# Reciprocal roots of norms, delta rule outputs and latent attention as one GpSimd power each

## The chip, the cores and the metric

One core of a Trainium2 chip runs the whole program. Its engines work side by side, each through its own list of instructions in order, and wait for one another by semaphores: TensorE (PE) multiplies matrices, VectorE (DVE) and ScalarE (ACT) do elementwise work, GpSimd (POOL) does elementwise work too, SyncE (SP) issues most of the DMAs. The metric is the time of one execution in microseconds on the device; lower is better.

## The reference

A trunk of two layers over 512 tokens of width 1024, all in fp32. Each layer adds a half-step feed-forward block, two token mixers side by side (a gated delta rule with 8 heads, and latent attention with 8 heads), and a second half-step feed-forward block. Root-mean-square norms stand everywhere:

```python
def rms_norm(x, gain):
    xf = x.astype(jnp.float32)
    y = xf * lax.rsqrt(jnp.mean(xf * xf, axis=-1, keepdims=True) + EPS)
    return (y * gain.astype(jnp.float32)).astype(x.dtype)
...
def gated_deltanet(qkv, z, ...):
    q, k = l2_norm(q), l2_norm(k)
    o = gated_delta_rule(q, k, v, g, beta)
    o = rms_norm(o, out_gain) * jax.nn.silu(z)
...
    t_inv = lax.linalg.triangular_solve(eye + m, ...)
...
def mla(...):
    q = (rms_norm(q_lat, q_lat_gain) @ w_q_up)
    kv = (rms_norm(kv_lat, kv_lat_gain) @ w_kv_up)
    q, k = rms_norm(q, q_norm), rms_norm(k, k_norm)
...
    for l in range(DEPTH):
        h = modulate(x, norm_ffn1[l], sh1, sc1)
        x = x + 0.5 * (1.0 + g1) * swiglu(h, ...)
        h = modulate(x, norm_mix[l], sh2, sc2)
        x = x + (1.0 + g2) * token_mix(h, ...)
        h = modulate(x, norm_ffn2[l], sh3, sc3)
        x = x + 0.5 * (1.0 + g3) * swiglu(h, ...)
```

## The kernel before

Activations lie feature by feature: 1024 features are 8 tiles of 128 partitions by 512 tokens. Every fp32 product is made of three matmuls (L94) of split operands: high by high, low by high, high by low. A weight slab arrives by DMA as `raw`, ScalarE rounds it to `whi` (L121), and VectorE subtracts that to get `wlo` (L122). A projection of 512 columns into the PSUM tile `acc` (three buffers) is 24 matmuls; behind it VectorE empties the accumulator, in the mixer with a causal convolution of three rows at L729 into `cv`.

The order of each engine's instructions is set by a scheduler that works through the program with priorities; a few stretches are pinned to the order of the code (the beginning, and the matmuls of some norms). So an edit that makes one row longer or shorter can change the order of other rows too.

Where reciprocal roots stand:

- **Begin** (L1446 to L1451). The first norm of the program: PE sums squares into `sm`, VectorE makes the variance `nv`, then a ScalarE square root, a VectorE reciprocal and one Newton round; PE spreads the result into `po`.
- **Norms** (`norm_scale`). Five later norms, each in two halves of 256 tokens. PE puts the sums of squares into `sm`, VectorE makes `nv` (128x2), `rsqrt` makes the root, PE spreads it into `po`. Between the two PE runs matmuls of a neighbouring projection.
- **Block inverse** (`invert`, once a layer). Before it, `key_system` runs once for each of the 8 heads: GpSimd adds a mask (L821) and multiplies (L823), VectorE forms `M` (L840), GpSimd copies its diagonal blocks (L842). GpSimd also makes the rotary products of the key (L1101 to L1122, tile `kr`). Then VectorE transposes the blocks (L855) and runs a forward substitution of 31 steps, each a product at L861 and a subtraction at L863. Meanwhile PE runs projections, whose accumulators VectorE empties between those steps. The tile `nh` (L1312 to L1315, 128x32) is the root of the keys' squared norms, made as a value times its reciprocal root; it is first used after the inverse.
- **Delta rule** (`gdn_tail`, 16 times: 8 heads, 2 layers). `sso` is the outputs' mean square, `som` its reciprocal root (128x4); the outputs `osb` are multiplied by it, transposed by PE and gated. The next head's chain of products with copies on VectorE (L1005, L1014) runs beside it.
- **Latent attention** (`mla_make`, 8 times: 4 pairs of heads, 2 layers). `ss` holds the mean squares of queries and keys, `scl` the 16 reciprocal roots; the key tiles `A` are scaled (L1202) and transposed by PE into `sm` (L99). The makes of pairs 1 to 3 stand within the attention of the pair ahead. The latent norm's root `rkv` (128x4) is made once a layer.

`rsqrt` without a table takes ten VectorE rows: a first guess from the bits of the number (L334) and three Newton rounds (L337 to L339). With a table it is a ScalarE square root (L331), a VectorE reciprocal (L332) and one round.

Of the kernel before, what the change touches and what calls it, by code (L numbers as in the profile page):

```python
# [62 lines left out]

BUFS = {
# [3 lines left out]
}  # L68

# [4 lines left out]
class Trunk:  # L74
# [119 lines left out]
    def setup(self):  # L194
        nc = self.nc
        self.one = self.t("ones", [P, 1])
        nc.vector.memset(self.one, 1.0)
        self.ones = self.one[:].to_broadcast([P, P])
        self.x = self.t("M", [P, KT, SEQ])
        self.condb = self.t("kph", [P, D])  # L200
        for k in range(0, KT, 2):
            nc.sync.dma_start(self.x[:, k:k + 2, :], self.ap["x"][:, k:k + 2, :])
        ct = self.t("ct", [P, KT])
        nc.sync.dma_start(ct, self.ap["c"])
        nc.sync.dma_start(self.condb, self.ap["crow"].to_broadcast([P, D]))
        self.cond = self.t("cond", [P, KT])
        self.const = self.t("const", [P, N_CONST])
        self.ident = self.const[:, C_ID:C_ID + P]
        self.neg = self.const[:, C_NEG:C_NEG + P]
        self.negt = self.const[:, C_NEGT:C_NEGT + P]  # L210
        nc.sync.dma_start(self.ident, self.ap["consts"][:, C_ID:C_ID + P])
        return ct
# [110 lines left out]
            nc.scalar.activation(sq[:, a:b], self.x[:, k, a:b], AF.Square)  # L323
            nc.vector.tensor_add(self.ss[:, a:b], self.ss[:, a:b], sq[:, a:b])

    def rsqrt(self, out, a, table=True):

        nc = self.nc
        n = out.shape[-1]
        if table:  # L330
            nc.scalar.activation(out, a, AF.Sqrt)  # L331
            nc.vector.reciprocal(out, out)  # L332
        else:
            nc.vector.tensor_scalar(out.bitcast(I32), a.bitcast(I32), -0.5, float(0x5F3759DF), ALU.mult, ALU.add)  # L334
        t = self.t("nr", [P, NI])[:, :n]
        for _ in range(1 if table else 3):
            nc.vector.scalar_tensor_tensor(t, out, -0.5, out, ALU.mult, ALU.mult)  # L337
            nc.vector.tensor_mul(t, t, a)
            nc.vector.scalar_tensor_tensor(out, t, 1.5, out, ALU.add, ALU.mult)  # L339

    def norm_scale(self, cols):

        nc = self.nc
        a, b = cols
        n = (b - a) // P
        ps = self.p("sm", [P, n, P])
        for i in range(n):
            self.mm(ps[:, i, 0:1], self.ss[:, a + i * P:a + (i + 1) * P], self.one, start=True, stop=True)
        var, rn = self.t("nv", [P, NT])[:, :n], self.t("nv", [P, NT])[:, :n]
        nc.vector.tensor_scalar(var, ps[:, :, 0], 1.0 / D, EPS, ALU.mult, ALU.add)  # L350
        self.rsqrt(rn, var, False)
        yield
        rb = self.p("po", [P, n, P])
        for i in range(n):
            self.mm(rb[:, i, :], rn[:, i:i + 1].to_broadcast([P, P]), self.ident, start=True, stop=True)
        yield rb[:].rearrange("p t c -> p (t c)")
# [674 lines left out]
    def gdn_tail(self, vec, st):  # L1031
# [3 lines left out]
        a, m = st["sso"], self.t("som", [P, NT])  # L1035
        nc.vector.tensor_scalar(ssq, ssq, EPS, EPS * P, ALU.add, ALU.mult)
        nc.vector.scalar_tensor_tensor(a, a, 1.0 / P, ssq, ALU.mult, ALU.add)
        self.rsqrt(m[:], a[:], False)
        nc.vector.tensor_mul(osb, osb, m[:].unsqueeze(2).to_broadcast([P, NT, P]))
        yield  # L1040
        ot = self.p("po")
# [83 lines left out]
    def mla_make(self, l, pr, lat, mla, st):  # L1125
# [59 lines left out]
        nc.vector.tensor_mul(ss[:, 1], ss[:, 1], b2(mla["rkv2"][:]))  # L1185
        nc.vector.tensor_add(ss[:, 1], ss[:, 1], b2(mla["kpe"][:]))
        scl = self.t("scl", [P, 2, NT, 2])
        self.rsqrt(scl[:].rearrange("p a t h -> p (a t h)"), ss[:].rearrange("p a t h -> p (a t h)"), False)
        nc.vector.tensor_scalar(scl[:, 0], scl[:, 0], QK ** -0.5, None, ALU.mult)
        rk = self.t("rk", [P, NT, 2])  # L1190
        nc.vector.tensor_mul(rk, scl[:, 1], b2(mla["rkv"][:]))
# [75 lines left out]
    def mix(self, l, vec, gate, finish, ws, ahead):  # L1267
# [42 lines left out]

        nh = gt["nh"]
        nc.vector.tensor_scalar(nh, gt["ssk"], 4.0 * EPS, None, ALU.add)  # L1312
        rs = self.t("s1", [P, NI])
        self.rsqrt(rs[:], nh[:])
        nc.vector.tensor_mul(nh, nh, rs)  # L1315
        tt = self.t("A", [P, NI, P])
        for i, _ in enumerate(self.invert(mall, diag, tt)):
            self.fill(FILL_INVERT[i])
# [109 lines left out]
    def begin(self, ct, vec, mod):  # L1428
# [13 lines left out]
        ordered(nc.scalar.activation(self.cond, ct, AF.Silu))  # L1442
        ordered(nc.scalar.activation(self.condb, self.condb, AF.Silu))
        nc.scalar.dma_start(self.ap["spill_c"], self.condb)
        var, rn, t = (self.t(n, [P, NT]) for n in ("nv", "nv", "nr"))
        ordered(nc.vector.tensor_scalar(var, ps[:, :, 0], 1.0 / D, EPS, ALU.mult, ALU.add))  # L1446
        ordered(nc.scalar.activation(rn, var, AF.Sqrt))
# [3 lines left out]
        ordered(nc.vector.scalar_tensor_tensor(rn, t, 1.5, rn, ALU.add, ALU.mult))  # L1451
# [218 lines left out]
```

## Time and profile before

| what | value |
|---|---|
| three runs, us | 2736.4, 2739.33, 2739.42 |
| median, us | 2739.33 |
| the profiled execution, us | 2742.08 |
| its span, us | 2740.3 |
| mean granted clock of TensorE | 0.998 |
| DMA over the span | 394.66 MB, 144 GB/s |

The span is what the profile's rows cover, from the first to the last instruction; the execution's own time lies 1.8 us above it. A row of the timeline gives the start and the length in microseconds, the engine, the line, the operation, the output and its inputs, and in brackets the idle time of that engine ahead of the row and what ended it. Where a matmul is concerned, starts are more exact than ends.

The steps of a root as they stand in the trace of before:

```profile
L337 DVE SCALAR_TENSOR_TENSOR nr<-som x48: 152/161/239, 585.1 to 2092.7; 128x4 f32<-128x4 f32 x48
L337 DVE SCALAR_TENSOR_TENSOR nr<-nv x30: 149/161/164, 378.0 to 2394.7; 128x2 f32<-128x2 f32 x30
L337 DVE SCALAR_TENSOR_TENSOR nr<-scl x24: 165/172/177, 750.2 to 2256.3; 128x16 f32<-128x16 f32 x24
L337 DVE SCALAR_TENSOR_TENSOR nr<-s x2: 192/192/192, 471.8 to 1828.0; 128x32 f32<-128x32 f32 x2
```

The three numbers are the shortest, the median and the longest duration in ns: a step takes some 0.16 us for up to 4 columns and 0.19 for 32.

### The profile page before, as it was taken

What the parts mean: (1) busy time and instruction counts of PE and PEld (TensorE: products, weight loads), DVE (VectorE), ACT (ScalarE), POOL (GpSimd) and SP (SyncE); (2) the same over time, 40 slices, a digit from 0 to 9 for tenths busy, and PEclk for the clock granted to TensorE, in tenths of its full rate; (3) what the DMA queues carried; (4) which work ended last, traced back from release to release, by engine and by line L of the source; (5) the groups of instructions that cost most, each with busy time, mean ns of one, the idle gap of its engine ahead of it and who ended that gap; (6) DMA issues with size and microseconds to landing.
All of it is one profiled execution on the core that took longest, in us unless ns stands there. A gap on an engine that the chain in (4) does not pass through costs nothing.

```text
span 2740.3 us, 44511 instructions
## 1 busy us (share of the span) xinstructions
PE 2695.0 (98%) x17168; PEld 2396.7 (87%) x17168; DVE 2006.5 (73%) x4025; ACT 1285.4 (47%) x2519; POOL 266.9 (10%) x390
## 2 busy tenths in 40 slices
PE   7999999999999999999999999999999999999999
PEld 6989988788888788998889999887888888898988
DVE  6877877777668767875678878786767686685755
ACT  5534345444446535443445344545434564453533
POOL 0000015000001011000010000150000111110000
PEclk9999999999999999999999999999999999999999
DMA  8678733222222453885528777322222224456642
GB/s 308 184 224 236 239 125 111 90 69 81 67 79 71 131 177 114 247 232 146 158 67 229 244 231 235 97 100 89 74 81 71 76 78 125 156 153 185 161 131 86
DMA packets 118869, 394.66 MB, mean 144 GB/s; under 512 B 13440, under 2 KB 16128, under 8 KB 118656
## 3 DMA queue, kind: packets, MB, share of 16 engines
q1 hardware_dynamic: 106128, 350.38, 38.7%
q0 software_dynamic: 10080, 36.70, 7.5%
q10 hardware_dynamic: 2448, 4.72, 0.4%
q8 instruction: 135, 2.21, 0.3%
q14 instruction: 78, 0.64, 0.1%
HBM read 376.55 MB, written 15.20 MB: 143 GB/s over the span
## 4 chain that ended last, share of the span: by engine, by line
PE 82%; DVE 9%; issue 3%; ACT 3%; POOL 2%; DMA 1%; SPq 0%; ACTq 0%; POOLq 0%; DVEq 0%
PE acc L94 57%; PE sc L94 16%; PE sm L94 5%; PE sm L99 2%; DVE wlo L122 2%; PE po L94 1%; DVE cv L729 1%; DVE L L861 1%; DVE L L863 1%; POOL g L821 0%; ACT whi L121 0%; POOL g L823 0%; POOL O L842 0%; DMA raw<-in_w_in 0%; ACT hhi L389 0%
## 5 line engine op out<-in xcount | busy, mean ns | idle before, releaser
L121 ACT CAST whi<-raw 128x512 fp32r<-128x512 f32 (+2 forms) x554 | 320.0, 607 | 429.2 <-PE acc L94 241.1
L94 PE MATMUL acc<-hhi,whi 128*128 128x512 f32 (+1 forms) x1368 | 506.3, 371 | 11.1 <-DVE cv L729 5.8
L94 PE MATMUL acc<-hlo,whi 128*128 128x512 f32 (+1 forms) x1368 | 487.6, 357 | 1.2 <-POOL hlo L392 0.3
L94 PE MATMUL acc<-hhi,wlo 128*128 128x512 f32 (+1 forms) x1368 | 486.7, 356 | 0.0
L122 DVE TENSOR_TENSOR wlo<-raw,whi 128x512 fp32r<-128x512 f32 (+2 forms) x554 | 387.9, 719 | 107.8 <-ACT whi L121 101.0
L94 PE MATMUL acc<-O,whi 128*128 128x512 f32 x1472 | 456.3, 391 | 2.7 <-ACT O L135 2.2
L94 PE MATMUL acc<-A,whi 128*128 128x256 f32 (+1 forms) x1808 | 346.6, 291 | 0.7 <-ACT g L653 0.5
L94 PEld LDWEIGHTS acc<-O,whi 128*128 128x128 f32 x1472 | 275.9, 188 | 60.4 <-ACT O L135 2.6
L94 PEld LDWEIGHTS acc<-hhi,whi 128*128 128x128 f32 x1368 | 259.5, 190 | 42.4 <-issue 8.3
L94 PEld LDWEIGHTS acc<-hhi,wlo 128*128 128x128 f32 x1368 | 259.4, 190 | 37.3 <-DVE wlo L1491 0.2
L94 PEld LDWEIGHTS acc<-A,whi 128*128 128x128 f32 x1808 | 286.0, 192 | 6.2 <-ACT g L653 0.9
L94 PEld LDWEIGHTS acc<-hlo,whi 128*128 128x128 f32 x1368 | 260.3, 190 | 31.7 <-POOL hlo L392 3.0
L94 PE MATMUL acc<-O,wlo 128*128 128x512 f32 x736 | 287.3, 390 | 0.0
L94 PE MATMUL acc<-A,wlo 128*128 128x256 f32 (+1 forms) x904 | 262.6, 290 | 0.0
L582 ACT CAST whi<-L 128x1024 fp32r<-128x1024 f32 x140 | 147.0, 1050 | 205.0 <-issue 77.0
L583 DVE TENSOR_TENSOR wlo<-L,whi 128x1024 fp32r<-128x1024 f32 x140 | 171.3, 1224 | 35.3 <-ACT whi L582 34.6
L94 PEld LDWEIGHTS acc<-A,wlo 128*128 128x128 f32 x904 | 173.3, 192 | 2.5
L269 DVE SCALAR_TENSOR_TENSOR L<-L,kph 128x1024 f32<-128x1024 f32 x142 | 169.9, 1220 | 5.0 <-DMA L<-in_ada_w 5.0
L583 DVE TENSOR_TENSOR wlo<-raw,whi 128x1024 fp32r<-128x1024 f32 x105 | 128.6, 1224 | 59.1 <-ACT whi L582 58.1
L557 POOL DMA_DIRECT2D L<-in_ffn_w x70 | 61.1, 873 | 1086.0 <-DMA L<-in_ffn_w 459.7
L582 ACT CAST whi<-raw 128x1024 fp32r<-128x1024 f32 x105 | 110.2, 1049 | 118.9 <-PE acc L94 49.3
L94 PEld LDWEIGHTS acc<-O,wlo 128*128 128x128 f32 x736 | 138.5, 188 | 28.9
(432 smaller groups left out, 5339.5 us busy)
## 6 DMA issues: line engine op xcount, KB each, us to landing
raw<-in_ffn_w SPq DMA_DIRECT2D x166, 512.0 KB, 4.3
L<-in_ada_w SPq DMA_DIRECT2D x142, 512.0 KB, 5.0
raw<-in_w_in SPq DMA_DIRECT2D x108, 512.0 KB, 3.4
L<-in_ffn_w SPq DMA_DIRECT2D x105, 512.0 KB, 4.5
L<-in_ffn_w POOLq DMA_DIRECT2D x70, 512.0 KB, 8.4
raw<-in_w_branch_a SPq DMA_DIRECT2D x16, 512.0 KB, 3.4
raw<-in_w_branch_b SPq DMA_DIRECT2D x16, 512.0 KB, 3.7
raw<-in_w_out SPq DMA_DIRECT2D x16, 512.0 KB, 3.5
```

Source lines behind the costliest of these rows:

```text
L94: i = self.nc.tensor.matmul(*a, **k)
L99: i = self.nc.tensor.transpose(*a, **k)
L121: nc.scalar.copy(hi[:, s], raw[:, s])
L122: nc.vector.tensor_sub(lo[:, s], raw[:, s], hi[:, s].bitcast(F32))
L269: self.order(self.nc.vector.scalar_tensor_tensor(raw, raw, 1.0, self.condb, ALU.mult, ALU.mult, accum_out=mod[:, o:o + 1]))
L557: nc.gpsimd.dma_start(t, w13[l, m2, half2].rearrange("p w k c -> p (w k c)"), accum_op=ALU.add)
L582: nc.scalar.copy(hi, t)
L583: nc.vector.tensor_sub(lo, t, hi[:].bitcast(F32))
L729: nc.vector.scalar_tensor_tensor(acc[:, s:], ps[:, :SEQ - s], w[j], acc[:, s:], ALU.mult, ALU.add)
L861: nc.vector.tensor_mul(tv, f[:, j + 1:, j:j + 1].to_broadcast([P, n, w]), x[:, j:j + 1, :w].to_broadcast([P, n, w]))
L863: nc.vector.tensor_sub(x[:, j + 1:, :w], x[:, j + 1:, :w], tv)
```

## The change

`rsqrt` becomes a single GpSimd `tensor_tensor` with the operation power, whose second operand is a constant -0.5 broadcast from a new tile `power`; VectorE fills that tile once at the start. The roots of `begin` go the same way, and `nh` becomes a power with +0.5. There are 39 powers: 1 of 128x4 at the beginning, 10 of 128x2 in the norms, 2 of 128x32 for `nh`, 16 of 128x4 for the delta rule, 2 of 128x4 for the latents, and 8 of 128x16 for attention. VectorE's list falls from 3711 to 3335 rows, GpSimd's grows from 347 to 386, ScalarE loses 6 (square roots and their table loads). The work buffers `nr` go.

```diff
+        self.power = self.t("power", [P, 2])
+        nc.vector.memset(self.power[:, 0:1], -0.5)
+        nc.vector.memset(self.power[:, 1:2], 0.5)
...
-    def rsqrt(self, out, a, table=True):
-
-        nc = self.nc
-        n = out.shape[-1]
-        if table:
-            nc.scalar.activation(out, a, AF.Sqrt)
-            nc.vector.reciprocal(out, out)
-        else:
-            nc.vector.tensor_scalar(out.bitcast(I32), a.bitcast(I32), -0.5, float(0x5F3759DF), ALU.mult, ALU.add)
-        t = self.t("nr", [P, NI])[:, :n]
-        for _ in range(1 if table else 3):
-            nc.vector.scalar_tensor_tensor(t, out, -0.5, out, ALU.mult, ALU.mult)
-            nc.vector.tensor_mul(t, t, a)
-            nc.vector.scalar_tensor_tensor(out, t, 1.5, out, ALU.add, ALU.mult)
+    def rsqrt(self, out, a):
+
+        self.nc.gpsimd.tensor_tensor(out, a, self.power[:, 0:1].to_broadcast([P, a.shape[-1]]), ALU.pow)
...
         nc.vector.tensor_scalar(nh, gt["ssk"], 4.0 * EPS, None, ALU.add)
-        rs = self.t("s1", [P, NI])
-        self.rsqrt(rs[:], nh[:])
-        nc.vector.tensor_mul(nh, nh, rs)
+        nc.gpsimd.tensor_tensor(nh, nh, self.power[:, 1:2].to_broadcast([P, NI]), ALU.pow)
...
-        var, rn, t = (self.t(n, [P, NT]) for n in ("nv", "nv", "nr"))
+        var, rn = (self.t("nv", [P, NT]) for _ in range(2))
         ordered(nc.vector.tensor_scalar(var, ps[:, :, 0], 1.0 / D, EPS, ALU.mult, ALU.add))
-        ordered(nc.scalar.activation(rn, var, AF.Sqrt))
-        ordered(nc.vector.reciprocal(rn, rn))
-        ordered(nc.vector.scalar_tensor_tensor(t, rn, -0.5, rn, ALU.mult, ALU.mult))
-        ordered(nc.vector.tensor_mul(t, t, var))
-        ordered(nc.vector.scalar_tensor_tensor(rn, t, 1.5, rn, ALU.add, ALU.mult))
+        self.rsqrt(rn, var)
```

The other three calls of `rsqrt` lose only their `False`. The lines of the changed kernel are lower by 8 in the functions behind `rsqrt` (L813 and L815 are the old L821 and L823, L834 the old L842).

The scheduler orders several engines anew. First GpSimd in layer 0, ahead of the block inverse. Before:

```order
L821 TENSOR_TENSOR g_4664<-g_4664,const_73 128x512
L1121 TENSOR_TENSOR g_4691<-g_3987,g_4680 128x4x32
L1122 TENSOR_TENSOR kr_4686<-kr_4686,g_4691 128x256
L823 TENSOR_TENSOR g_4664<-g_4664,kap_4039 128x512
L842 COPY O_4043<-M_4042 32x128 x4
```

And of the change, at the same place:

```order
L813 TENSOR_TENSOR g_4642<-g_4642,const_76 128x512
L1113 TENSOR_TENSOR g_4669<-g_3965,g_4658 128x4x32
L1305 TENSOR_TENSOR nh_4019<-nh_4019,power_63 128x32
L1114 TENSOR_TENSOR kr_4664<-kr_4664,g_4669 128x256
L815 TENSOR_TENSOR g_4642<-g_4642,kap_4017 128x512
L834 COPY O_4021<-M_4020 32x128 x4
```

The power of `nh` now stands ahead of the product at L815, whose result VectorE needs for the last `M`, and so ahead of the copies that the transpose waits for.

Second, VectorE up to the first group of convolutions within the substitution. The width of a step (175, 192, ...) tells how far the substitution has come. Before:

```order
L861 TENSOR_TENSOR L_4710<-L_4708,L_4709 128x156
L863 TENSOR_TENSOR L_4709<-L_4709,L_4710 128x26x6
L122 TENSOR_TENSOR wlo_4854<-raw_4852,whi_4853 128x512
L729 SCALAR_TENSOR_TENSOR cv_4801<-acc_4766,vec_75,cv_4801 128x509
L861 TENSOR_TENSOR L_4710<-L_4708,L_4709 128x175
```

And of the change, from the same point of the substitution:

```order
L853 TENSOR_TENSOR L_4681<-L_4679,L_4680 128x156
L855 TENSOR_TENSOR L_4680<-L_4680,L_4681 128x26x6
L122 TENSOR_TENSOR wlo_4780<-raw_4778,whi_4779 128x512
L853 TENSOR_TENSOR L_4681<-L_4679,L_4680 128x175
L855 TENSOR_TENSOR L_4680<-L_4680,L_4681 128x25x7
L853 TENSOR_TENSOR L_4681<-L_4679,L_4680 128x192
L855 TENSOR_TENSOR L_4680<-L_4680,L_4681 128x24x8
L853 TENSOR_TENSOR L_4681<-L_4679,L_4680 128x207
L855 TENSOR_TENSOR L_4680<-L_4680,L_4681 128x23x9
L853 TENSOR_TENSOR L_4681<-L_4679,L_4680 128x220
L122 TENSOR_TENSOR wlo_4825<-raw_4823,whi_4824 128x512
L721 SCALAR_TENSOR_TENSOR cv_4772<-acc_4737,vec_78,cv_4772 128x509
```

The convolution that empties the accumulator (L729, now L721) stands behind 20 steps of the substitution instead of 14. The weight split `wlo_4780` is the old `wlo_4809`, whose first half stood ahead of the transpose and now stands behind it, so 4 splits instead of 2 lie between the transpose and this convolution. By the fourth group both orders have done 62 steps and 16 splits.

Third, PE within attention, in layer 0 at the make of the second pair. The tiles are the raw keys `A` and their rotary part `s`, transposed into `sm`. Before (the projection `acc_8202` has 12 matmuls at this place):

```order
L94 MATMUL sc_8218<-kph_7338,c_1218_7337 128x256
L94 MATMUL sc_8218<-c_1221_7340,c_1218_7337 128x256
L94 MATMUL acc_8202<-hhi_3718,whi_8187 128x512
L94 MATMUL acc_8202<-hlo_3719,whi_8187 128x512
L94 MATMUL acc_8202<-hhi_3718,wlo_8188 128x512
...
L94 MATMUL po_8064<-g_8184,A_7335 128x128 x2
L99 MATMUL sm_8231<-const_73,A_7888 128x128 x2
L99 MATMUL sm_8231<-const_73,s_1375_8170 128x128
L99 MATMUL sm_8240<-const_73,A_7888 128x128 x2
```

And of the change:

```order
L94 MATMUL sc_8079<-kph_7219,c_1205_7218 128x256
L94 MATMUL sc_8079<-c_1208_7221,c_1205_7218 128x256
L99 MATMUL sm_8092<-const_76,A_7759 128x128 x2
L99 MATMUL sm_8092<-const_76,s_1360_8031 128x128
L99 MATMUL sm_8101<-const_76,A_7759 128x128 x2
L94 MATMUL acc_8063<-hhi_3706,whi_8048 128x512
L99 MATMUL sm_8101<-const_76,s_1361_8035 128x128
L94 MATMUL acc_8063<-hlo_3707,whi_8048 128x512
```

The key transposes move ahead of the 12 matmuls of the projection. Elsewhere PE's work is the same in nearly the same order; in the second halves of the norms 4 matmuls stand between the sums and the use of the root where 17 stood, and in the first halves still 30 or more. SyncE's list keeps its 702 rows, with two neighbouring loads exchanged once a layer.

More of the change, by code (lines that the diff above doesn't have):

```diff
@@ L65 @@
     "raw": 2, "wlo": 3, "whi": 3, "hhi": 1, "hlo": 1, "A": 2, "O": 8, "M": 1, "L": 5, "c3": 5, "cv": 3, "g": 7,
[1 row of a table removed]
+    "s1": 6, "vec": 2, "mod": 2, "nv": 4, "sc4": 2, "ssq": 2, "sso": 2, "som": 2, "s2": 2, "mx": 4, "smx": 4,
     "ss": 2, "scl": 2, "rk": 2, "acc": 3, "sm": 2, "sc": 2, "po": 1,
@@ L350, in norm_scale @@
         nc.vector.tensor_scalar(var, ps[:, :, 0], 1.0 / D, EPS, ALU.mult, ALU.add)
-        self.rsqrt(rn, var, False)
+        self.rsqrt(rn, var)
         yield
@@ L1037, in gdn_tail @@
         nc.vector.scalar_tensor_tensor(a, a, 1.0 / P, ssq, ALU.mult, ALU.add)
-        self.rsqrt(m[:], a[:], False)
+        self.rsqrt(m[:], a[:])
         nc.vector.tensor_mul(osb, osb, m[:].unsqueeze(2).to_broadcast([P, NT, P]))
@@ L1187, in mla_make @@
         scl = self.t("scl", [P, 2, NT, 2])
-        self.rsqrt(scl[:].rearrange("p a t h -> p (a t h)"), ss[:].rearrange("p a t h -> p (a t h)"), False)
+        self.rsqrt(scl[:].rearrange("p a t h -> p (a t h)"), ss[:].rearrange("p a t h -> p (a t h)"))
         nc.vector.tensor_scalar(scl[:, 0], scl[:, 0], QK ** -0.5, None, ALU.mult)
@@ L1352, in mix @@
                                     (("rkv", NT), ("rkv2", NT), ("kpe", NT), ("qms", NT), ("gqk", 1)))
-        self.rsqrt(rkv[:], ms[:, 1, :], False)
+        self.rsqrt(rkv[:], ms[:, 1, :])
         nc.vector.tensor_mul(rkv2, rkv, rkv)
@@ L1444, in begin @@
         nc.scalar.dma_start(self.ap["spill_c"], self.condb)
-        var, rn, t = (self.t(n, [P, NT]) for n in ("nv", "nv", "nr"))
+        var, rn = (self.t("nv", [P, NT]) for _ in range(2))
         ordered(nc.vector.tensor_scalar(var, ps[:, :, 0], 1.0 / D, EPS, ALU.mult, ALU.add))
-        ordered(nc.scalar.activation(rn, var, AF.Sqrt))
-        ordered(nc.vector.reciprocal(rn, rn))
-        ordered(nc.vector.scalar_tensor_tensor(t, rn, -0.5, rn, ALU.mult, ALU.mult))
-        ordered(nc.vector.tensor_mul(t, t, var))
-        ordered(nc.vector.scalar_tensor_tensor(rn, t, 1.5, rn, ALU.add, ALU.mult))
+        self.rsqrt(rn, var)
         rp = self.p("po", [P, NT, P])
```

1 row of the table BUFS is left out of this document.

## The prediction

> **What bounds the kernel now.** I read the page from the top: the engines' shares, then the chain that ended last, then what PE waits for.
>
> ```profile
> span 2740.3 us, 44511 instructions
> PE 2695.0 (98%) x17168; PEld 2396.7 (87%) x17168; DVE 2006.5 (73%) x4025; ACT 1285.4 (47%) x2519; POOL 266.9 (10%) x390
> PE 82%; DVE 9%; issue 3%; ACT 3%; POOL 2%; DMA 1%; SPq 0%; ACTq 0%; POOLq 0%; DVEq 0%
> ...
> PE acc L94 <- DVE cv L729: 5.8, 6, 1.8
> ...
> PE sm L99 <- DVE A L1202: 2.5, 6, 0.5
> ...
> PE po L94 <- DVE nv L339: 0.9, 5, 0.2
> PE po L99 <- DVE rkv L339: 0.9, 2, 0.4
> ```
>
> PE is busy 98% of the span, so time is gained or lost only where PE stands still. The rows of the second list (microseconds in all, times, the longest) are those behind which a reciprocal root stands: 10.1 us together, and 2.0 more at the very beginning (below). The change also removes about 380 VectorE instructions, but VectorE has 27% to spare, so their busy time is worth nothing by itself. What counts is when five kinds of results arrive, and which queue they pass.
>
> The sum is made against the profiled execution (2742.08 us, span 2740.3) and then carried to the median of the runs, 2739.33, which is 2.75 us lower.
>
> **The price of a power.** No power stands in the trace. The nearest rows are GpSimd's products:
>
> ```profile
> L1089 POOL TENSOR_TENSOR s<-cv,c 128x64 f32<-128x64 f32 x32 | 10.3, 323 | 0.0
> ...
> L1122 POOL TENSOR_TENSOR kr<-kr,g 128x256 f32<-128x256 f32 x2 | 1.5, 738 | 0.2
> ```
>
> 64 columns take 323 ns and 256 take 738: 2.16 ns a column and about 0.18 us fixed. Low bound: a power costs as much as one product, 0.19 us for 2 or 4 columns, 0.22 for 16, 0.25 for 32. High bound: the ten steps of the old root as ten GpSimd products, 1.9 us for 2 or 4 columns, 2.2 for 16, 2.5 for 32. I take one fixed part and 25 steps of 2.16 ns for each column (a logarithm, a product and an exponential, each about as long as the old chain of ten): **0.29 us for 2 columns, 0.40 for 4, 1.06 for 16, 1.94 for 32**. For few columns that is near the product, for many near the ten. The spare steps are my choice; both ends go into the range.
>
> **Begin.** The very first norm has no matmul to hide behind.
>
> ```profile
> 13.13 1.28 ACT L1447 ACT_TABLE_LOAD   x1 [0.40 <-ACT kph L1443]
> 13.53 0.16 DVE L1446 TENSOR_SCALAR nv<-sm 128x4 f32<-128x4 f32 x1 [1.96 <-PE sm L94]
> ...
> 15.48 2.08 PE L94 MATMUL po<-const,nv 128*128 128x128 f32 x8 [1.99 <-DVE nv L1451]
> ...
> 27.94 0.79 PE L94 MATMUL acc<-hhi,whi 128*128 128x512 f32 x1 [2.31 <-ACT whi L1490]
> ```
>
> The variance is there at 13.69; the root waits for ScalarE's table (until 14.41), then takes a square root, a reciprocal and a round, and PE goes at 15.48. With a power PE goes at 13.69 + 0.07 (the handoff to GpSimd) + 0.40 + 0.05 = 14.21, 1.27 earlier. Behind it come VectorE's conditioning products, whose slots release the weights' DMAs, and those set the first projection at 27.94; some of the lead may be lost there: **-1.1** (from -1.3 at the low price to +0.3 at the high one).
>
> **Norms.** The first halves have 30 or more matmuls of about 0.12 us between the sums and the use, longer than any price here: nothing. The second halves have 17 of them before and 4 after (the rows of the change):
>
> ```profile
> 389.06 0.16 DVE L350 TENSOR_SCALAR nv<-sm 128x2 f32<-128x2 f32 x1 [1.19 <-PE sm L94]
> ...
> 389.32 0.28 PE L94 MATMUL acc<-hhi,whi 128*128 128x256 f32 x1
> ...
> 390.87 0.28 PE L94 MATMUL acc<-hlo,whi 128*128 128x256 f32 x1
> 391.33 0.68 PE L94 MATMUL po<-const,nv 128*128 128x128 f32 x4 [0.18 <-DVE nv L339]
> ```
>
> Matmuls there start 0.12 apart, so without a wait this one would start at 390.99; it loses 0.34. After the change the fourth matmul behind the sums, that of 389.32, ends the cover, and the next would start at 389.44. The power is ready for PE at 389.22 + 0.07 + 0.29 + 0.15 (as from the end of the old chain, 391.18, to 391.33) = 389.73, a loss of 0.29. Five times -0.05: **-0.3** (low -0.8; high 5 x 1.56 = +7.8).
>
> **Block inverse, once a layer: the main term.** Here the change puts the power of 32 columns into GpSimd's queue, ahead of the last product of the key system, L823:
>
> ```profile
> 475.97 1.04 POOL L823 TENSOR_TENSOR g<-g,kap 128x512 f32<-128x512 f32 x1
> 477.80 1.67 POOL L842 COPY O<-M 32x128 f32<-32x128 f32 x4 [0.79 <-DVE M L840]
> ...
> 477.04 0.69 DVE L840 TENSOR_TENSOR M<-sc,g 128x512 f32<-128x512 f32 x1 [3.89 <-POOL g L823]
> ...
> 479.51 2.11 DVE L855 STREAM_TRANSPOSE L<-O 128x1024 f32<-128x1024 f32 x1 [1.18 <-POOL O L842]
> ```
>
> GpSimd runs without a gap up to L823, VectorE waits 3.89 us for it, and the solve begins at 479.51 when GpSimd's copies are in. The old root's reciprocal, round and product lay inside those 3.89 us of idle VectorE and were free. The power lies in front of L823, so the solve starts later by all of it: 1.94. From there VectorE has no slack:
>
> ```profile
> 488.90 0.47 PE L94 MATMUL acc<-hhi,whi 128*128 128x512 f32 x1 [0.50 <-DVE cv L729]
> ...
> 490.33 0.38 DVE L863 TENSOR_TENSOR L<-L,L 128x207 f32<-128x207 f32 x1
> ...
> 491.05 0.68 DVE L122 TENSOR_TENSOR wlo<-raw,whi 128x512 fp32r<-128x512 f32 x1
> ...
> 500.66 0.47 PE L94 MATMUL acc<-hhi,whi 128*128 128x512 f32 x1 [0.61 <-DVE cv L729]
> ...
> 500.00:520.00 20.00, 19.39 (x86) 16.00 (x86) 19.14 (x43) 7.53 (x14) 0.00 (x0) 1.00 0.30 104
> ...
> 524.46 0.47 PE L94 MATMUL acc<-hhi,whi 128*128 128x512 f32 x1 [1.76 <-DVE cv L729]
> ...
> 1880.63 0.47 PE L94 MATMUL acc<-hhi,whi 128*128 128x512 f32 x1 [1.80 <-DVE cv L729]
> ```
>
> (In the window the numbers are its length and the busy us of PE, weight loads, VectorE, ScalarE and GpSimd: VectorE 19.14 of 20.) The scheduler has also dealt VectorE's rows anew. Before the first group of convolutions stand 14 solve steps and 2 weight splits (L122) now; after, 20 and 4. Six steps of some 0.38 and two splits of 0.68, as in the rows above, make 3.6 us. The accumulator which PE awaits at 488.90 is freed 3.6 + 1.94 = 5.5 later; the weight splits moved behind the transpose make PE stop earlier for a part of that, which changes the place of the idle time, not its sum. Later the same PE gains the waits it had: 0.61 at 500.66 and 1.76 at 524.46, since it arrives late itself. Net 5.5 - 2.4 = **3.1 in each layer**, 1.2 of it from the new order alone.
>
> Then the clock:
>
> ```profile
> 368.00:374.00 6.00, 4.20 (x23) 4.23 (x24) 4.01 (x10) 1.20 (x3) 0.00 (x0) 0.72 0.50 176
> ...
> 520.00:526.00 6.00, 4.24 (x19) 3.20 (x19) 4.28 (x6) 4.79 (x6) 0.00 (x0) 1.00 0.27 87
> ...
> 1880.00:1886.00 6.00, 5.37 (x66) 4.01 (x68) 3.27 (x6) 5.28 (x9) 0.00 (x0) 0.72 0.35 107
> ```
>
> Behind PE's idle time of 2.16 us (to 369.80) and of 1.80 (to 1880.63) the granted clock is 0.72 over 6 us, a loss of 6 x 0.28 = 1.7; behind 1.76 (to 524.46) it stays 1.00. An idle time of some 5 us will lower it in layer 0 too: **+1.7**; in layer 1 the dip only changes place. The Trainium skill, "TensorE: Matmul & The Clock Gate", section "HAM oscillation — how this bites in real kernels", puts the limit at gaps over about 3.4 us; by it, with the idle time in pieces, there would be no dip after the change and the sum would be 3.4 lower. The trace dips at 1.80 already, so I keep the 1.7.
>
> Block inverse together 2 x 3.1 + 1.7 = **+7.9** (low price 4.6, high 9.1).
>
> **Delta rule's outputs, 16 heads.** PE does not wait anywhere in this stretch. VectorE's row that waits for the power stands in front of a copy which PE needs:
>
> ```profile
> 604.51 0.16 DVE L1037 SCALAR_TENSOR_TENSOR sso<-sso,ssq 128x4 f32<-128x4 f32 x1 [0.47 <-ACT sc L1028]
> ...
> 605.00 0.28 DVE L1005 TENSOR_SCALAR s<-sc 128x128 f32<-128x128 f32 x1
> ...
> 606.14 0.38 PE L94 MATMUL sc<-s,L 128*128 128x128 f32 x2
> ```
>
> The power would be ready at 604.67 + 0.07 + 0.40 + 0.03 = 605.17, then the scaling product (0.69) holds the copy until 606.14: just at the edge, in 6 heads; in the other 10 the copy comes first and about 1 us is spare. **+0.3** (low 0; high 6 x 1.5 + 10 x 0.9 = +18). The last head's root and that of the latent norm end 0.44 late twice in the list (rkv L339); a power of 0.40 for a chain of 2 us removes that: **-0.9** (high 0).
>
> **Attention, 6 makes of keys inside it.**
>
> ```profile
> 812.80 0.15 DVE L1186 TENSOR_TENSOR ss<-ss,kpe 128x8 f32<-128x8 f32 x1
> ...
> 813.47 0.28 DVE L1244 TENSOR_SCALAR g<-g,smx 128x128 f32<-128x128 f32 x1
> ...
> 816.93 0.17 DVE L1189 TENSOR_SCALAR scl<-scl 128x8 f32<-128x8 f32 x1
> ...
> 814.08 0.40 PE L94 MATMUL acc<-hhi,whi 128*128 128x512 f32 x1
> ...
> 817.81 0.41 PE L99 MATMUL sm<-const,A 128*128 128x128 f32 x2 [0.40 <-DVE A L1202]
> ```
>
> The chain used to be hidden: 3.98 us from the sums to L1189, under a projection. Now the key transposes stand where 814.08 is. Keys: 812.95 + 0.07 + 1.06 + 0.03 = 814.11, and 0.88 more (816.93 to 817.81): 814.99, a wait of 0.91 in place of 0.40. 6 x 0.51 = **+3.1**. At the low price VectorE's own rows ahead (a split and a scaling, to 813.75) leave 0.15 each, +0.9; at the high, 6 x 1.65 = +9.9. The two makes ahead of attention keep their PE order and over 3 us of cover: nothing.
>
> **Sum:** -1.1 - 0.3 + 7.9 + 0.3 - 0.9 + 3.1 = **+9.0**: 2751.1 in the profile's terms, 2748.3 against the median.
>
> **Rivals.**
> *A cheap power* (one product): -1.3 - 0.8 + 4.6 + 0 - 0.9 + 0.9 = +2.5, 2741.8. For it: a fixed 0.18 us is most of a small GpSimd row. Against: a root is not one step on an engine with 2.16 ns a column for a product.
> *A dear power* (ten products, or a fixed cost that the products do not have): 0.3 + 7.8 + 9.1 + 18 + 0 + 9.9 = +45, 2784. For it: nothing in the trace excludes it.
> *Faster:* the solve's first convolution is not later. Place: 479 to 489 and the like in layer 1. If GpSimd's queue ahead of the solve became shorter by the 3.6 + 1.94 that I charge, PE would not stop at 489, the waits of 1.76 and 1.80 and the dip would go: -5.3, with begin, norms, latent norm and cheap keys -1.4: -6.7, 2732.6. It decides from about 3.7 us a layer (the sum of 9.0 without its 1.7 of clock, halved); below that the change still loses. Against: those products remain, and a row is added.
> *A load of code:* the power is GpSimd's first arithmetic, at 13.7.
>
> ```profile
> 73.86 1.29 POOL L477 TENSOR_TENSOR c<-cv,c 128x512 f32<-128x512 f32 x1 [16.44 <-DVE c L475]
> ```
>
> Now the first is at 73.86, takes no longer than its like, and had 16.44 us of idle time to hide a load in; at 13.7 there is less. At the price of the one load in the trace (ScalarE's table, 1.28) begin would be +0.2: 2749.6. The Trainium skill, "GPSIMD Engine Reference", section "Instruction dispatch", puts the first call of a freshly loaded kernel at about 6 us; by it the time would be 2754. Against: the load can be issued before the input arrives.
>
> **How the numbers follow.** Forecast 0.54 (its own range 2744 to 2756, 13 to 40 steps a column), cheap 0.22, dear 0.14, faster 0.05, code load 0.05. A measurement here tells about 0.2%, 5.5 us, from no change: within it lie the cheap case and the foot of the forecast, 0.27; faster 0.05; slower 0.68. The range leaves out the faster case and most of the dear one: 2739 to 2776.
>
> **What would show it.** GpSimd's rows of the powers give the price at 2, 4, 16 and 32 columns at once: about 0.3, 0.4, 1.1 and 1.9. PE's wait near 489 and 1845 should be 4 to 6 us in sum, with clock below 1 behind it, and those near 524 and 1880 gone. The transposes of the keys should wait some 0.9, six times. The first group's matmuls should begin about 1.1 before 27.94. The prediction is wrong if the power has a large fixed cost (then the 16 heads and the norms pay), or if PE's wait at the first convolution stays near 0.5.

## The result and the profile after

| | before | after |
|---|---|---|
| median, us | 2738.4 (4 runs, 2736.4 to 2739.42) | 2775.64 (4 runs, 2773.66 to 2778.08) |
| ratio, 95% interval | | 1.014, 1.0124 to 1.0156 |
| span of the profiled execution, us | 2740.3 | 2776.3 |

One execution of before beside e5 to e8 (2926.74 us) and one of e7 (5373.55 us) lie far above all others of their kernels and are left out below.

The change costs 37 us where 9 were forecast. Three lines of the page after (the span, the engines' shares, the chain that ended last), and lines from the list of what PE waits for (us in all, times, the longest):

```profile
span 2776.3 us, 44171 instructions
PE 2703.6 (97%) x17168; PEld 2406.8 (87%) x17168; DVE 1953.7 (70%) x3653; ACT 1276.4 (46%) x2510; POOL 330.3 (12%) x429
PE 80%; DVE 7%; issue 4%; POOL 4%; ACT 3%; DMA 2%; POOLq 0%; ACTq 0%; DVEq 0%; SPq 0%
...
PE sm L99 <- DVE A L1194: 17.7, 6, 3.0
...
PE acc L94 <- DVE wlo L122: 9.7, 2, 4.9
PE acc L94 <- DVE cv L721: 5.5, 4, 1.4
PE po L94 <- POOL nv L331: 4.7, 6, 2.4
PE sc L94 <- DVE s L997: 3.2, 6, 0.6
```

VectorE did get lighter (2006.5 to 1953.7 us), but PE's waits grew. The wait for the keys in attention went from 2.5 to 17.7; the wait for the copy `s`, which stands behind the scaling of the heads, is new, and so is PE's wait for a weight split, 4.9 us twice.

The powers themselves, grouped by shape (line, engine, operation, names, shape, count, busy us, mean ns, idle before):

```profile
L331 POOL TENSOR_TENSOR scl<-ss,power 128x16 f32<-128x16 f32 x8 | 25.5, 3192 | 36.1 <-DVE ss L1178 36.1
...
L331 POOL TENSOR_TENSOR som<-sso,power 128x4 f32<-128x4 f32 x16 | 16.2, 1014 | 478.0 <-DVE sso L1029 439.6 <-DVE ms L1070 38.4
...
L1305 POOL TENSOR_TENSOR nh<-nh,power 128x32 f32<-128x32 f32 x2 | 10.9, 5452 | 0.0
...
L331 POOL TENSOR_TENSOR nv<-nv,power 128x2 f32<-128x2 f32 x10 | 7.1, 707 | 236.7 <-DVE nv L342 236.7
...
L331 POOL TENSOR_TENSOR nv<-nv,power 128x4 f32<-128x4 f32 x1 | 2.1, 2084 | 13.7 <-DVE nv L1436 13.7
```

A power takes 0.71 us for 2 columns, 1.01 for 4 and 5.45 for 32: some 0.158 us a column ((5.45 - 0.71) / 30) and 0.4 fixed. A GpSimd product takes 2.16 ns a column, so a power costs 73 products a column, not 25.

To see where the time went, the starts of the same matmuls in both profiles are compared. PE's **lag** is the start in one profile minus the start before, as the median of 25 neighbouring matmuls; how much it grows across a stage is what the stage costs. Two layers together, in us, for the change and for the runs below (each is described there). This table is called the ledger. A sum in it moves by up to about 0.5 us with the place of a stage's borders, and each column rests on one profiled execution of either kernel:

| stage | after | e1 | e2 | e3 | e4 | e5 | e8 |
|---|---|---|---|---|---|---|---|
| block inverse | 12.8 | 4.3 | -1.5 | 13.1 | 13.4 | 3.5 | -1.8 |
| delta rule's heads | 4.7 | 0.0 | 4.6 | 4.7 | 0.0 | 4.6 | -0.1 |
| attention | 23.2 | -1.6 | 19.3 | 0.1 | 22.4 | 23.3 | 0.0 |
| five norms | -4.7 | -7.4 | | | | -4.6 | -4.7 |

The last row takes in the feed-forward block behind the third norm. There before has two waits of PE for `g` (0.3 us each, 1583 to 1605), which the change and e8 do not have: 1.5 of the change's 4.7 and 1.1 of e8's.

The rest of the change's 35.9 us of lag at the end is +1.1 at the beginning and -1.5 at the border of the layers, where before has a lowered clock behind a wait of 2.21 us and the change, behind 2.3 us at the same place, has not; what is left, +0.3, is scattered.

**The block inverse after**, layer 0: timeline rows of GpSimd, VectorE and PE, and the row of one window (length; busy us of PE, weight loads, VectorE, ScalarE, GpSimd; granted clock; DMA):

```profile
475.94 5.46 POOL L1305 TENSOR_TENSOR nh<-nh,power 128x32 f32<-128x32 f32 x1
482.07 1.03 POOL L815 TENSOR_TENSOR g<-g,kap 128x512 f32<-128x512 f32 x1
...
483.14 0.69 DVE L832 TENSOR_TENSOR M<-sc,g 128x512 f32<-128x512 f32 x1 [10.84 <-POOL g L815]
...
489.04 0.79 PE L94 MATMUL acc<-hhi,wlo 128*128 128x512 f32 x1 [4.87 <-DVE wlo L122]
...
490.00:496.00 6.00, 6.00 (x19) 4.72 (x18) 5.69 (x16) 0.00 (x0) 0.00 (x0) 0.67 0.28 89
```

L815, the product that VectorE waits for, starts at 482.07 instead of 475.97, and VectorE's idle time ahead of `M` grows from 3.89 to 10.84. PE stops for the weight split that the new order puts behind the transpose, 4.87 us, and runs on at a clock of 0.67. In both layers the clock is 0.50 for 6.8 us there (487.19 to 494.01 and 1859.34 to 1866.17).

**Attention after**, one of the six makes:

```profile
823.40 3.29 POOL L331 TENSOR_TENSOR scl<-ss,power 128x16 f32<-128x16 f32 x1 [4.91 <-DVE ss L1178]
...
826.72 0.17 DVE L1181 TENSOR_SCALAR scl<-scl 128x8 f32<-128x8 f32 x1 [2.60 <-POOL scl L331]
...
827.61 0.41 PE L99 MATMUL sm<-const,A 128*128 128x128 f32 x2 [3.02 <-DVE A L1194]
...
828.00:834.00 6.00, 6.00 (x27) 4.91 (x26) 5.09 (x20) 2.26 (x8) 0.00 (x0) 0.72 0.00 0
```

The transposes wait 3.02 us where they waited 0.40, and the clock is 0.72 over the 6 us behind: 6 x 0.28 = 1.7 us more.

**One head of the delta rule after**:

```profile
613.82 0.69 DVE L1031 TENSOR_TENSOR g<-g,som 128x512 f32<-128x512 f32 x1 [1.12 <-POOL som L331]
614.43 0.28 DVE L997 TENSOR_SCALAR s<-sc 128x128 f32<-128x128 f32 x1
...
614.86 0.46 PE L94 MATMUL sc<-s,L 128*128 128x128 f32 x2 [0.52 <-DVE s L997]
```

VectorE stands idle for 1.12 us ahead of the scaling, the copy `s` comes behind it, and PE waits for the copy: 6 times, 0.5 to 0.6 us.

### The profile page after: what moved, and what is told of

It is laid out like the page before. It is cut to its first block, busy times and chain, and to the rows that moved or that the text cites. A ratio compares the mean times of both kernels' runs of the same rounds, so it can differ in the third digit from the quotient of the medians.

```text
span 2776.3 us, 44171 instructions
## 1 busy us (share of the span) xinstructions
PE 2703.6 (97%) x17168; PEld 2406.8 (87%) x17168; DVE 1953.7 (70%) x3653; ACT 1276.4 (46%) x2510; POOL 330.3 (12%) x429
## 3 DMA queue, kind: packets, MB, share of 16 engines
q8 instruction: 135, 2.21, 0.3%
## 4 chain that ended last, share of the span: by engine, by line
PE 80%; DVE 7%; issue 4%; POOL 4%; ACT 3%; DMA 2%; POOLq 0%; ACTq 0%; DVEq 0%; SPq 0%
PE acc L94 55%; PE sc L94 16%; PE sm L94 5%; PE sm L99 2%; DVE wlo L122 1%; PE po L94 1%; DVE cv L721 1%; POOL g L813 1%; POOL scl L331 1%; DVE L L853 1%; ACT whi L121 1%; DVE L L855 1%; POOL g L815 1%; POOL O L834 1%; DMA raw<-in_w_out 1%
## 5 line engine op out<-in xcount | busy, mean ns | idle before, releaser
L94 PE MATMUL acc<-hhi,whi 128*128 128x512 f32 (+1 forms) x1368 | 512.5, 375 | 7.9 <-DVE cv L721 5.5
```

What stands on the lines that cost most here:

```text
L94: i = self.nc.tensor.matmul(*a, **k)
```

## The experiments

Two theories. **Theory 1:** the length of a power, at the places where it stands on PE's path, makes the loss. **Theory 2:** the new order and the trips through GpSimd's queue make it, whatever the row takes.

### e1: products in the place of the powers

The product leaves the roots out; the orders of all engines are those of the change.

```diff
-        nc.vector.memset(self.power[:, 0:1], -0.5)
-        nc.vector.memset(self.power[:, 1:2], 0.5)
+        nc.vector.memset(self.power[:, 0:1], 0.125)
+        nc.vector.memset(self.power[:, 1:2], 0.125)
...
-        self.nc.gpsimd.tensor_tensor(out, a, self.power[:, 0:1].to_broadcast([P, a.shape[-1]]), ALU.pow)
+        self.nc.gpsimd.tensor_tensor(out, a, self.power[:, 0:1].to_broadcast([P, a.shape[-1]]), ALU.mult)
...
-        nc.gpsimd.tensor_tensor(nh, nh, self.power[:, 1:2].to_broadcast([P, NI]), ALU.pow)
+        nc.gpsimd.tensor_tensor(nh, nh, self.power[:, 1:2].to_broadcast([P, NI]), ALU.mult)
```

> The changed kernel with a GpSimd product by 0.125 in the place of each of the 39 powers (so the roots are left out; every engine's order is that of the changed kernel). In the changed kernel a power takes 0.71 us for 2 columns, 1.01 for 4, 3.2 for 16 and 5.45 for 32, and PE is behind by 36 us at the end: 12.8 of it at the two block inverses, 23.2 in attention, 4.7 in the delta rule, about 1 at the beginning, less some 5 elsewhere. Theory 1 (the length of the power does it): the block inverses come down to about 2.4 in sum, attention to about 1, the delta rule to 0 or below; the whole 2737 to 2744. Theory 2 (the new order and the trips to GpSimd's queue do it, whatever the length of the row): 2760 or more, the block inverses still over 8 and attention over 12.

Measured: 2735.01 us, ratio to before 0.9981 (0.9971 to 0.9990), 2 us under the range of theory 1. The same program with short rows is even a little faster than before, so theory 2 falls: the order and the trips cost nothing in sum. The ledger shows it stage by stage: attention 23.2 to -1.6, the heads 4.7 to 0.0, the block inverse 12.8 to 4.3 (2.4 were expected). What stays at the inverse is the new order of VectorE's rows; PE waits there for the first convolution (list of PE's waits in e1):

```profile
PE acc L94 <- DVE cv L721: 7.3, 2, 3.7
```

Twice 3.7 us, against 0.5 at this place before, less the later waits, which are gone: 7.3 in all against 5.8. The rest is the clock. It is 0.50 from 490.36 to 497.19 and from 1842.04 to 1848.87, where the two inverses of before have one stretch at 0.50, 3.4 us long.

### e2: `nh` the old way

```diff
-        nc.gpsimd.tensor_tensor(nh, nh, self.power[:, 1:2].to_broadcast([P, NI]), ALU.pow)
+        rs = self.t("s1", [P, NI])
+        self.rsqrt_old(rs[:], nh[:])
+        nc.vector.tensor_mul(nh, nh, rs)
```

(`rsqrt_old` is the function of before under a new name, here and below.)

> The changed kernel with nh made the old way (ScalarE root, VectorE reciprocal, round and product); the order of VectorE in the forward substitution falls back to that of before with it. Theory 1: the power of 5.45 us and the new order are gone from the block inverse, 11 to 13 us less than the changed kernel, 2763 to 2765. Theory 2 (of the order alone): the same order comes back, so the same 11 to 13; this run does not tell the two apart, it tells both from theory 3 (the new waits are spread and the projections behind absorb them, or the clock's dips make most of it): less than 6 us.

Measured: 2760.26 us, 15.4 less than the change, more than the 11 to 13 expected. The inverse's 12.8 us go entirely (-1.5 in the ledger: the dip of the clock in layer 1 of before is absent in this profile); theory 3 of the expectation falls. This profile also shows what the clock adds in attention, where the six waits are still 3 us each. Windows of 6 us behind the first and the second of them, and four shorter ones that are explained below:

```profile
817.74:823.74 6.00, 6.00 (x35) 4.92 (x36) 5.81 (x23) 2.75 (x9) 0.00 (x0) 1.00 0.00 0
861.00:867.00 6.00, 6.00 (x28) 5.13 (x29) 5.32 (x22) 2.26 (x8) 0.00 (x0) 0.73 0.00 0
...
813.04:816.46 3.42, 1.69 (x12) 1.40 (x10) 1.19 (x5) 1.19 (x3) 2.92 (x1) 1.00 0.21 58
816.46:819.87 3.41, 2.13 (x12) 1.73 (x13) 2.98 (x13) 0.09 (x1) 0.37 (x1) 1.00 0.00 0
...
857.42:860.83 3.41, 0.65 (x4) 0.40 (x3) 0.81 (x6) 0.26 (x1) 2.66 (x1) 1.00 0.21 58
860.83:864.24 3.41, 3.24 (x11) 2.80 (x12) 3.35 (x14) 0.83 (x3) 0.00 (x0) 0.50 0.00 0
```

The same wait lowers the clock at one make and not at another. The lag grows by 2.2 us over the first make (0.50 to 2.70) and by 3.5 over the second (2.70 to 6.24). In the change all six makes have 0.72, and each costs 3.7 to 4.2.

The traces' record of the clock shows what decides. Each dip is a clock of 0.50 over one or two stretches of 3.41 us, and within a run the starts of the dips lie whole multiples of 3.41 us apart. Cut along these stretches (the four shorter windows), the wait of the first make falls on both sides of a border: PE is busy 1.69 and 2.13 us of 3.41, and no dip follows. That of the second lies in one stretch: PE is busy 0.65 us, and the next stretch has 0.50. Behind the first 40 us of all eleven profiles, every dip began behind a stretch in which PE was idle for about 1.8 us or more; one such stretch (1.91 us, in e6) had no dip behind it.

### e3: `scl` the old way

```diff
-        self.rsqrt(scl[:].rearrange("p a t h -> p (a t h)"), ss[:].rearrange("p a t h -> p (a t h)"))
+        self.rsqrt_old(scl[:].rearrange("p a t h -> p (a t h)"), ss[:].rearrange("p a t h -> p (a t h)"), False)
```

> The changed kernel with the 8 roots scl of attention by the old ten VectorE rows. Theory 1: attention's 23.2 us go, about 2752. If VectorE's relief by the other powers is worth something in attention, a little less than before there (lag falling by up to 2 us); if the stall in attention were the clock or the moved transposes alone, a part of the 23 would stay.

Measured: 2753.15 us, 22.5 less than the change, and attention costs 0.1 in the ledger. No dip is left at the six makes: the clock there is 1.00. So the relief that the other powers give VectorE shows no gain in attention.

### e4: `som` and `rkv` the old way

```diff
-        self.rsqrt(m[:], a[:])
+        self.rsqrt_old(m[:], a[:], False)
...
-        self.rsqrt(rkv[:], ms[:, 1, :])
+        self.rsqrt_old(rkv[:], ms[:, 1, :], False)
```

> The changed kernel with the 16 roots som of the delta rule and the 2 latent roots rkv by the old ten VectorE rows. Theory 1: 16 powers of 1.01 us stand in front of copies that PE needs in some heads; 4.7 us of lag in two layers go, 2771. If instead the 1.01 us is hidden and the lag comes from the heads' order, nothing changes (2775).

Measured: 2773.83 us, 1.8 less than the change where 4.7 were expected. By time alone this is inconclusive (the two ranges overlap). In the ledger the heads' 4.7 us are gone (0.0), so the term stands; the profile's span is 3.0 shorter, and the rest is within what dips of the clock move from one execution to the next: this profile has one dip more than the change's, at 1372 on the border of the layers (1.7 us).

### e5: the power of `nh` behind the copies

```diff
-        nc.gpsimd.tensor_tensor(nh, nh, self.power[:, 1:2].to_broadcast([P, NI]), ALU.pow)
...
         for i, _ in enumerate(self.invert(mall, diag, tt)):
+            if i == 0:
+                half = self.t("half", [P, 1])
+                nc.vector.tensor_scalar(half, self.f[:, 0, 0:1], 0.0, 0.5, ALU.mult, ALU.add)
+                nc.gpsimd.tensor_tensor(nh, nh, half[:].to_broadcast([P, NI]), ALU.pow)
             self.fill(FILL_INVERT[i])
```

(`self.f` is the transposed block tile that `invert` makes.)

> The changed kernel with the power of nh made to wait for the transpose (its exponent is a VectorE row of 128x1 behind the transpose), so that the power stands behind the last copies in GpSimd's queue instead of ahead of the last product; the power is as long as before and VectorE's and PE's orders stay those of the changed kernel but for that row. Theory 1 (the 5.45 us count because they stand ahead of the solve): the block inverses fall from 12.8 to about 4.3, as with the product, 2765 to 2768. Theory 2 (a long GpSimd row slows VectorE's solve wherever it runs beside it): the lag stays over 10 and the time over 2772; the solve's steps beside the power would be longer than 0.2 to 0.3 us.

Measured: 2765.65 us, 10 less than the change. The same power, as long as ever, costs nothing behind the chain; the 3.5 us left are about those of the new order in e1 (4.3). GpSimd's and VectorE's rows at that place:

```profile
481.37 5.51 POOL L1311 TENSOR_TENSOR nh<-nh,half 128x32 f32<-128x32 f32 x1 [2.48 <-DVE L L854]
...
481.62 0.22 DVE L854 TENSOR_TENSOR L<-L,L 128x60 f32<-128x60 f32 x1
...
482.30 0.69 DVE L122 TENSOR_TENSOR wlo<-raw,whi 128x512 fp32r<-128x512 f32 x1
```

VectorE's rows that run beside the power are as long as before (0.22 and 0.68): this power, while it runs, does not slow them.

### e6: the price by itself

```diff
+        base = self.t("pb", [P, 4, 8])
+        for i, v in enumerate((1.0, 3.7, 3.7e-6, 3.7e6)):
+            nc.vector.memset(base[:, i], v)
+        po = self.t("pbo", [P, 6, 16])
+        for i, (src, e, w) in enumerate(((base[:, 0, 0:1], 0, 1), (base[:, 0], 0, 8), (base[:, 1], 0, 8),
+                                         (base[:, 1], 1, 8), (base[:, 2], 0, 8),
+                                         (base[:, 0:2].rearrange("p a b -> p (a b)"), 0, 16))):
+            nc.gpsimd.tensor_tensor(po[:, i, 0:w], src, self.power[:, e:e + 1].to_broadcast([P, w]), ALU.pow)
```

> The changed kernel with six more GpSimd powers at its start, on constants: 128x1 of 1.0 (the first of the program), then 128x8 of 1.0, of 3.7, of 3.7 with exponent +0.5, of 3.7e-6, and 128x16 half of 1.0 and half of 3.7. If the price is 0.40 us and 0.15 to 0.16 us for each column whatever the value: 1.6 us for 8 columns four times, and 2.9 for 16. If it depends on the value, the rows of 8 differ from one another by over 0.1 us. If the first power of the program pays 1.07 us for being first (2.08 against 1.01 for 4 columns), 128x1 takes 1.6 instead of 0.55, and the power of the beginning then takes 1.01 in place of 2.08.

One run, 2772.05 us; only its rows are used. The first powers of 1, 8 and 16 columns, and the power of the beginning:

```profile
1.04 0.57 POOL L209 TENSOR_TENSOR pbo<-pb,power 128x1 f32<-128x1 f32 x1 [0.60 <-DVE pb L204]
1.59 1.65 POOL L209 TENSOR_TENSOR pbo<-pb,power 128x8 f32<-128x8 f32 x1
8.01 2.88 POOL L209 TENSOR_TENSOR pbo<-pb,power 128x16 f32<-128x16 f32 x1
13.92 2.06 POOL L339 TENSOR_TENSOR nv<-nv,power 128x4 f32<-128x4 f32 x1 [3.02 <-DVE nv L1444]
```

The four rows of 8 columns follow one another at 1.59, 3.22, 4.82 and 6.41, 1.6 us each: neither the value nor the sign of the exponent matters for these. The price is 0.41 + 0.155 us a column. The first power of the program takes 0.57, what the line gives for one column, so nothing is paid for being first; and the power of the beginning takes 2.06 although six stood ahead of it. So the 1.07 us more than elsewhere are not for being first; e9 finds the reason.

### e8 and e7: powers only where the ledger gains

In e8 the kernel before has powers in the ten half norms; e7 adds the root of the beginning. Both also have one idle power of a single column at the program's start.

```diff
+        self.power = self.t("power", [P, 1])
+        nc.vector.memset(self.power, -0.5)
+        warm = self.t("warm", [P, 1])
+        nc.gpsimd.tensor_tensor(warm, self.one, self.power, ALU.pow)
...
+    def gpow(self, out, a):
+
+        self.nc.gpsimd.tensor_tensor(out, a, self.power[:].to_broadcast([P, a.shape[-1]]), ALU.pow)
...
-        self.rsqrt(rn, var, False)
+        self.gpow(rn, var)
```

And in e7 besides, in place of the five rows of the beginning's root:

```diff
+        self.gpow(rn, var)
```

> The kernel before with the ten roots of the norms' halves as powers and nothing else. Theory 1: 4 to 5 us less than before, 2734 to 2735, the wait of PE for hhi (2.9 us, three times) gone, and a wait for the power of about 0.45 at each second half in its place. If the norms' part is as I predicted it (a wait of about the old length in place of the old one, nothing behind it): 2738 to 2741.

> The kernel before with powers only where the ledger of the changed kernel shows a gain: the ten roots of the norms' halves (128x2), and the root of the beginning with an idle 128x1 power at the start of the program ahead of it. In the changed kernel PE's lag falls by 4.7 us in sum at the five norms although PE waits there for the power; expected from theory 1: 4 to 5 less than before from the norms, 0.6 from the beginning, 2733 to 2735. If the gain at the norms came from other rows (an order that the other powers bring), 2738 or more.

Measured: e8 2734.43 us, ratio to before 0.9984 (0.9976 to 0.9993); e7 2733.22, 0.9981 (0.9972 to 0.9990). Both are faster than before (2738.86 in the same series), by 4.4 and 5.6 us, about as expected. The gain at the norms comes from their own powers, since e8 changes nothing else that is used. (The -1.8 of e8 at the inverse in the ledger is, as in e2, a dip of before's profile that this profile lacks.) The gain isn't at the power, for which PE waits (PE's list in e8; the row and the list of before):

```profile
PE po L94 <- POOL nv L347: 2.2, 5, 0.4
...
1039.30 0.39 PE L94 MATMUL acc<-hhi,whi 128*128 128x256 f32 x1 [0.87 <-ACT hhi L389]
...
PE acc L94 <- ACT hhi L389: 2.9, 3, 1.1
```

Five waits of 0.44 have taken the place of five of 0.18. But before, PE stopped again 1.8 us behind `po` in three of the five norms, for the normalized activations (0.87, 1.11, 0.87). In e8, as in the change, the root comes ahead of 13 matmuls that used to cover the old chain, so these now cover ScalarE's and VectorE's work behind it, and the second stop is gone. By these lists that is 2.9 us less and 1.3 more; the feed-forward block adds its 1.1 to 1.5. The rest of the 4.7, about 2 us, was not followed.

### e9: the power of the beginning without a VectorE row beside it

```diff
         self.gpow(rn, var)
+        seen = self.t("seen", [P, 1])
+        ordered(nc.vector.tensor_copy(seen, rn[:, 0:1]))
         rp = self.p("po", [P, NT, P])
```

> The kernel of e7 with one VectorE row of 128x1 that reads the beginning's root, pinned ahead of the first conditioning product (a row of 128x1024 that takes 1.22 us). In e7, as in the changed kernel, the power of the beginning starts 0.02 to 0.03 us behind that product and takes 2.08 us in place of 1.01, an idle power ahead of it changed nothing (e6), and with a product in its place it took 1.25 in place of 0.19 (e1). Theory: a GpSimd row that starts while such a VectorE row runs waits until it ends. Then the power takes 1.01 here, PE spreads the root 1.3 after the variance's row starts instead of 2.4, and PE's first projection begins 0.5 to 1 earlier against the variance; the time 2732 to 2734, not to be told from e7. If the 1.07 us belong to 128x4 powers of this place for another reason (the data, the DMAs at 400 GB/s), the power takes 2.08 again and everything is later by 0.8.

In e1 the VectorE row and the product at this place; then the power in e9, and PE behind the root in the change and in e9:

```profile
13.87 1.22 DVE L272 SCALAR_TENSOR_TENSOR L<-L,kph 128x1024 f32<-128x1024 f32 x1
13.90 1.25 POOL L331 TENSOR_TENSOR nv<-nv,power 128x4 f32<-128x4 f32 x1 [13.46 <-DVE nv L1436]
...
13.57 1.02 POOL L347 TENSOR_TENSOR nv<-nv,power 128x4 f32<-128x4 f32 x1 [12.01 <-DVE nv L1454]
...
13.84 0.16 DVE L1436 TENSOR_SCALAR nv<-sm 128x4 f32<-128x4 f32 x1 [1.96 <-PE sm L94]
16.23 2.08 PE L94 MATMUL po<-const,nv 128*128 128x128 f32 x8 [2.42 <-POOL nv L331]
...
13.33 0.16 DVE L1454 TENSOR_SCALAR nv<-sm 128x4 f32<-128x4 f32 x1 [1.96 <-PE sm L94]
14.65 2.08 PE L94 MATMUL po<-const,nv 128*128 128x128 f32 x8 [1.35 <-POOL nv L347]
```

With the VectorE row held back the power takes 1.02, and PE spreads the root 1.32 us after the variance's row starts (in the change 2.39). The first projection starts at 27.27; in e7 it was 28.18, before 27.94. The time, 2735.56 (ratio 0.9987, 0.9978 to 0.9996), lies 1.6 over the range expected, but is not to be told from e7's: 0.9 us is too little to show there.

## Why the prediction was wrong

- **The price of a power** is the step that failed. I took 25 steps of 2.16 ns a column and bounded it above by ten products; it is 73 products a column. For 2, 4, 16 and 32 columns I had 0.29, 0.40, 1.06 and 1.94; measured were 0.71, 1.01, 2.9 to 3.3 and 5.45. Nothing in the trace bounded it from above: ten VectorE steps do the same work by another method, and their number says nothing of GpSimd's. With the measured prices the prediction's own terms give +0.4 (beginning, 15.89 for 15.48) + 1.9 (norms) + 15.0 (inverse) + 3.7 (heads) + 16.4 (attention) = +37 (without the latent root's gain), the measured sum, but partly since two errors cancel, below. At the low price the terms did not come out: e1 is the cheap case built, 2741.8 by the prediction and 2735.0 measured.
- **The range:** 2775.6 lies just inside its upper end, 2776. That is luck: the forecast's own prices went up to 40 steps a column and the dear rival's to ten products, and for 16 and 32 columns the measured price is above both.
- **Block inverse:** the place was right. The power stands ahead of the key system's last product, and the solve starts later by nearly all of it; e5 shows that it is the place. The new order costs about what I gave it, 4.3 in e1, where the low price had 4.6, but not by the same sum: PE's waits grew less than I had it (1.5 instead of 2.9) and the clock fell in both layers and for longer, where I had one dip more in layer 0. Sized with 5.45 the term is 15.0, measured 12.8. Of the later waits that I took back, that at 524 was still there in layer 0 (1.40 at 532.45); in layer 1 it was gone.
- **Delta rule:** the mechanism was right to the number of heads, 6 waits behind the scaling; at 1.01 us instead of 0.40 each is 0.53 (3.2 / 6), and the ledger's 4.7 leaves about 0.25 each for the restart. The latent root's gain of 0.9 needs a short power: it is there in e1 (about 1.0 a layer) and gone in the change.
- **Attention:** 3.1 forecast, 23.2 measured. The wait has the place I gave it and the length of the power; what came on top is the clock. I charged a dip behind the inverse's wait and none here, where I had waits of 0.9; at the measured price they are 3 us, and at 0.72 over 6 us the dips cost 1.7 each. The first make of e2, with the wait and without a dip, costs 2.2: six of these and six dips are 13.2 + 10.2 = 23.4. I also let the length of a wait decide on a dip (1.80 against 1.76); it is the idle time within a stretch of 3.41 us, as e2 shows. The rule that I weighed, the Trainium skill's limit of gaps over about 3.4 us ("TensorE: Matmul & The Clock Gate", section "HAM oscillation — how this bites in real kernels"), would have no dip here; the trace has six behind waits of 2.9 to 3.0.
- **Norms:** the wait for the root grew as the price says, but I looked no further than that wait. The stop behind it, for `hhi`, fell away, which makes a part of the gain: -4.7 measured (1.5 of it in the feed-forward block), -0.3 forecast, +1.9 at the true price. This is the error of the other sign.
- **Beginning:** -1.1 forecast; the first projection came 0.75 late. Of this 0.31 was there before the root (the variance's row starts at 13.84, in before at 13.53); from that row on PE spreads the root after 2.39 us instead of 1.95, and the projection follows 0.44 later. The old order kept the conditioning product behind the root; the new one lets it run beside the power, which then waits for it.
- Of the rivals, the dear power was the right one in kind, with too low a price for 16 and 32 columns (2.2 and 2.5) and too high a one for 2 and 4 (1.9). The faster case needed GpSimd's queue ahead of the solve to become shorter; it became longer by the power. The code load did not show: the first power takes 0.57.

## What to carry to other kernels

Fewer instructions are no measure: for 16 columns one row of 2.9 to 3.3 us replaced ten of about 0.17 each. An operation that no row of the trace shows has no upper bound from rows of other operations; measure it by itself, on a few columns and on many, before it goes into a chain. Where a result comes earlier, follow the path past the first wait: what could be traced of the gain at the norms was at the second stop, not at the first.

## What the runs showed of the hardware

- A GpSimd power of fp32 on 128 partitions takes 0.41 us and 0.155 us a column, whatever the value or the sign of the exponent in e6.
- A GpSimd row that starts just behind certain VectorE rows waits for them; those seen here have two inputs in SBUF, and no run tried others. In e1 a product of 128x4 took 1.25 us beside a row of 1.22 and 0.20 in the heads; products of 128x16 took 0.60 beside a weight split and 0.22 alone, and the powers of 128x16 in the change 3.29 and 2.91 in the same places. With the row held back (e9) the power of the beginning took 1.02 instead of 2.08. The other way round nothing was seen: in e5 such VectorE rows ran at their usual length beside a power of 5.51. The Trainium skill, "SBUF — State Buffer", section "SBUF: two separate sides", says that whichever of the two starts first holds the shared ports for its whole instruction; the first half agrees with the 1.25 and 0.60, the second does not with e5.
- A wait of PE of 1.8 to 3 us lowers the granted clock to about 0.72 over the next 6 us in some places and in some executions not, at the same wait. In e2 a wait of 3.0 us that a border of the stretches of 3.41 us divided brought no dip, and one of 2.9 in a single stretch brought 0.50 over the next.
